# Query rows in tiles of the GLA stage, fetched a step ahead, and GLA keys turned through DRAM

## The chip, the cores and the metric

The kernel runs on one core of a Trainium2 chip. The metric is the device time of one execution in microseconds (us). Inputs and outputs are in DRAM, all in 32-bit floats.

## What is computed

One layer of a hybrid decoder for a prompt of 1024 tokens and, with the same weights, for eight decode queries ("samples") of one token each. One input projection feeds three branches; each is projected, gated, summed, and projected once more.

```python
h = rmsnorm(x, norm_gain)
proj = h @ w_in                     # 1024 x 10256
q, k, v, gla_g, a_lr, u, pool_g, xq, xg, merge = split(proj)
...
# A) gated linear attention, chunks of 64, 4 heads, key dim 128, value dim 256
q_dec, k_inv, k_end = qb * exp(b), kb * exp(-b), kb * exp(b_last - b)
att = where(mask, q_dec @ k_inv.T, 0)
o_intra, dS = att @ vb, k_end.T @ vb
S = decay * S + dS;  o = q_dec @ S_before + o_intra
# C) cross attention, 4 heads, head dim 256, 256 memory tokens
p = softmax((xq @ mk.T) * 256 ** -0.5);  o = p @ mv
```

For the prompt, the memory keys and values `mk`, `mv` are computed from `mem_prompt` and shared. For the samples each of the eight has its own keys and values in a cache, 256 tokens each per head. `k_end` is what the text calls the decayed keys: `dS` needs them with the token index on partitions, while the projection leaves them with the channel on partitions.

## The kernel before

**Main stream.** A product of two fp32 matrices is made of three fp32r matmuls of the parts "hi" and "lo" (`mm3`, L242 to L244; `split` makes the parts, hi on ScalarE, here ACT, L223, lo on VectorE, here DVE, L224). The input projection is cut in 40 pairs of 256 columns, each done by a Strassen-like scheme in seven products. A product has two halves, each of them twelve matmuls per group of 258 columns (tile `px`, six PSUM banks). Between the groups of the main stream the function `fill` may put side steps: first those of the memory keys, then the cross attention (`cross_steps`), then GLA (`gla_steps`), then pooling. A side step is what lies between two `yield`s; the number that it yields is its weight, and the weights are spread evenly over the main stream (WORK_A = 493 over about 330 places). So TensorE (PE) has one order, written out by hand, in which side steps and main groups alternate. SyncE (SP), which issues the loads, has program order too; the order of DVE, ACT and GpSimd (POOL) is set by a scheduler.

**Buffers.** Side matmuls write the tile `pz`, of which there are two PSUM banks. `R` is a ring of 14 tiles of 128x512 words for nearly all side data; `V` is a set of four such tiles; `raw` (three) takes the weights of the main stream from DRAM; `alc` and `st` are tiles of 128x256 words, two each, which the GLA stage uses for its gate input and its state.

**Samples in the cross stage.** `cross_sample` handles one head. `cross_scaled` and `cross_rows` turn the eight scaled queries and write them to DRAM (`xq_scr`). For each of four pairs of samples, `fetch` loads two tiles of keys `kc` (256 KB each) and a tile `qb` with the two query rows broadcast over all partitions, all from `V`. Four reduces on DVE (L777) multiply keys and row and sum them into `sc`. The next pair is fetched behind the reduces. Then `sc` is turned on TensorE (L791), the softmax makes `ps` (L793 to L798), `ps` is turned (L803) and copied into `pm`; two batches of four value tiles `vc` from `V` are multiplied by it (L817), the second loaded when the first has been used; the results are turned (`cs`).

The prompt's steps of the cross stage are `cross_memory` (turns the keys of a head, `mkT`, and splits the values), `cross_queries` (splits the queries, `xqs`), `cross_scores`, `cross_weights` (turns the weights, L724, and splits them, `pT`) and `cross_values`. `cross_steps` runs them over 16 chunks of 256 queries and takes one sub-step of the samples at each `yield next(samples, 0)`.

**GLA.** `gla_steps` runs over 16 chunks of 256 tokens (head h, chunk c), each in two parts of 128. `gla_load` fetches keys and queries two chunks ahead (`kq`), `gla_gates` makes the decayed keys (L935) and the other factors one chunk ahead, `gla_within` makes the masked 64x64 products of a part (L944, L945), turns the part's decayed keys on TensorE (L946) into the same bank, and splits both into `ak` (128x256, hi and lo). `gla_recur` multiplies `ak` with the values and updates the state (L963). The order within a chunk is: gates of the next one, within (even part), recur of the previous chunk's odd part, within (odd part), recur (even part), out.

Of the kernel before, what the change touches and what calls it, by code (L numbers as in the profile page):

```python
# [9 lines left out]
F32 = mybir.dt.float32  # L10
# [37 lines left out]
def trunk_kernel(ctx: ExitStack, tc: tile.TileContext,  # L48
# [159 lines left out]
    al_scr = scratch(2, "als", (P, HT))  # L208
    q_scr, k_scr = (scratch(2, s, PAIR) for s in ("qsc", "ksc"))
    vt_scr = scratch(NH, "vtsc", (T, DV))  # L210
    u_scr, xq_raw = (scratch(4, s, PAIR) for s in ("usc", "xqsc"))
    mix_scr = [None if n == 0 else scratch(4, f"mixsc{n}_", (P, 2, T)) for n in range(3)]
    on_scr = scratch(NH, "onsc", (DV // 32, 32, 2, 4, 2, 64))
# [539 lines left out]

    def cross_sample(h):

        if h == 0:
            cross_scaled(0)
            cross_rows(0)
            yield 1.2
            yield 0.5  # L760
            yield 0.5
        sc = wk.tile([P, 16], F32, tag="sc", name="sc", bufs=2)

        def fetch(b2):
            kc = [loaded(ck[2 * b2 + bb, :, h, :].rearrange("(a p) d -> p a d", p=P), [2, DV], "kc", V) for bb in range(2)]
            qb = V([2, DV], name="qb")
            nc.sync.dma_start(out=qb, in_=xq_scr[h][2 * b2:2 * b2 + 2].partition_broadcast(P))
            return kc, qb

        kcs, qb = fetch(0)  # L770
        yield 0.5
        yield 0.5
        for b2 in range(4):
            for bb in range(2):
                b, kc = 2 * b2 + bb, kcs[bb]
                for a in range(2):
                    nc.vector.tensor_tensor_reduce(kc[:, a, :], kc[:, a, :], qb[:, bb, :],  # L777
                                                   scale=1.0, scalar=0.0, op0=ALU.mult, op1=ALU.add,
                                                   accum_out=sc[:, a * NS + b:a * NS + b + 1])
            if b2 == 2 and h + 1 < NH:  # L780
                cross_scaled(h + 1)
            if b2 < 3:
                kcs, qb = fetch(b2 + 1)
                yield 1.2
            elif h + 1 < NH:
                cross_rows(h + 1)
            yield 1
# [44 lines left out]
    def cross_steps():  # L832
# [12 lines left out]

        samples = chain_of(cross_sample(h) for h in range(NH))
        cross_load(0)
        cross_memory(0)
        cross_fetch(0, 0)
        yield 2  # L850
        cross_queries(0, 0)
        cross_fetch(0, 1)
        for s in range(16 + 2):
            if s < 16:
                scores(s)
                yield 3
                if s + 1 < 16:
                    cross_queries(*divmod(s + 1, 4))
                if s + 2 < 16:
                    cross_fetch(*divmod(s + 2, 4))  # L860
            if s % 4 == 2 and s < 14:
                cross_load(s // 4 + 1)
            if s >= 1:
                yield next(samples, 0)
            if 0 <= s - 2:
                values(s - 2)
                yield 1.7
            if s >= 1:
                yield next(samples, 0)
            if s % 4 == 3 and s < 15:  # L870
                memory(s + 1)
                yield 2
            if 0 <= s - 1 < 16:
                weights(s - 1)
                yield 1.7
            for _ in range(3):
                if s >= 1:
                    yield next(samples, 0)
# [25 lines left out]
    def gla_gates(h, c):  # L904
# [29 lines left out]
        act(z, z, AF.Exp, scale=1.0 / TAU)  # L934
        nc.vector.tensor_tensor(k, k, z, op=ALU.mult)  # L935
        gla["g", h, c] = kq, kiqi, decp

    def gla_within(h, pr):

        c, cs = pr // 2, slice((pr % 2) * P, (pr % 2 + 1) * P)  # L940
        kq, kiqi, _ = gla["g", h, c]
        kt, qd, ki, qi = (x[:, cs] for x in (kq[:, 0], kq[:, 1], kiqi[:, 0], kiqi[:, 1]))
        t = PZ()
        nc.tensor.matmul(t[0:64, 0:P], lhsT=ki[:, 0:64], rhs=qi, start=True, stop=True)  # L944
        nc.tensor.matmul(t[64:P, 0:P], lhsT=ki[:, 64:P], rhs=qd, start=True, stop=True)  # L945
        nc.tensor.transpose(t[:, P:2 * P], kt, ident)  # L946
        nc.vector.copy_predicated(t[:, 0:P], nmask, zeros)
        ak = R([2, DV], F32R, name="ak")
        split(ak[:, 0], ak[:, 1], t[:, :DV])
        gla["w", h, pr] = ak[:, 0], ak[:, 1]  # L950

    def gla_recur(h, pr):
        c, cs = pr // 2, slice((pr % 2) * P, (pr % 2 + 1) * P)
        hi, lo = gla["w", h, pr]
        vh, vl = (x[:, pr % 2] for x in gla["vs", h, c])
        _, kiqi, decp = gla["g", h, c]
        st = gla.get(("st", h))
        t = PZ()
        td, to = t[:, :DV], t[:, DV:]
        mm3(td, hi[:, P:], lo[:, P:], vh, vl, True, True)  # L960
        mm3(to, hi[:, :P], lo[:, :P], vh, vl, True, st is None)
        if st is not None:
            nc.tensor.matmul(to, lhsT=kiqi[:, 1, cs], rhs=st, start=False, stop=True)  # L963
        s2 = wk.tile([P, DV], F32, tag="st", name="st", bufs=2)
# [104 lines left out]
    def gla_steps():  # L1069
# [7 lines left out]
        for n in range(N + 1):  # L1077
# [5 lines left out]
            if n < N:  # L1083
                gla_split(h, c)
                gla_within(h, 2 * c)
                yield 2
            if n > 0:
                gla_recur(ph, 2 * pc + 1)
                yield 2
                yield next(samples, 0)  # L1090
            if n < N:
                gla_within(h, 2 * c + 1)
                yield 2
                yield next(samples, 0)
# [471 lines left out]
```

## Time and profile before

| what | value |
| --- | --- |
| time, median of 3 runs | 1442.61 us (1440.45 to 1442.92) |
| time of the profiled run | 1445.01 us |
| its span, first to last instruction | 1443.3 us |
| mean granted TensorE clock | 0.997 |
| bytes moved by DMA | 259.42 MB, 180 GB/s on the mean |
| input projection with side steps | to about 1000 us |
| cross stage | about 120 to 380 us |
| GLA stage | about 385 to 740 us |
| transposes of decayed keys (L946) | 32, 10.5 us busy |

In the rows of the profile, a group or an instruction is named by its line, engine and operation, then by the tiles "out<-in"; `128*128 128x258` is a stationary operand of 128*128 and a moving one of 258 columns. What stands in brackets at a timeline row is the idle time of the engine ahead of it and what ended it. `SPq` is the queue in which SP issues DMAs, `PEld` the load of weights into TensorE. Rows of stretches give the window, its length, the busy time of PE, PEld, DVE, ACT and POOL with instruction counts, then the granted clock, the DMA share and GB/s. A row of waits gives the total, how often, and the longest. Tile rows give the shortest, median and longest duration in ns. DMA rows end with KB each and the median us from issue to landing.

### The profile page before, as it was taken

How to read it: one execution, taken by the hardware profiler on the slowest of the kernel's cores; microseconds unless marked ns; L12 is line 12 of the kernel's file. 1: busy time of each engine (PE TensorE's matmuls, PEld its weight loads, DVE VectorE, ACT ScalarE, POOL GpSimd, SP SyncE). 2: the span in 40 equal slices, each digit the busy share in tenths (PEclk: the TensorE clock that was granted, in tenths of full speed). 3: DMA queues.
4: the chain of work that ended last, by engine and by line, in shares of the span. 5: the costliest groups of instructions: out<-in, count | busy, mean ns of one | idle time of the engine just before them, and what ended most of it. 6: DMA issues, size and time to landing. Idle time of an engine off the chain costs nothing.

```text
span 1443.3 us, 28179 instructions
## 1 busy us (share of the span) xinstructions
PE 1417.4 (98%) x10689; PEld 1356.1 (94%) x10689; DVE 916.2 (63%) x2123; ACT 679.0 (47%) x1575; POOL 222.1 (15%) x401
## 2 busy tenths in 40 slices
PE   8999999999999999999999999999999999999998
PEld 6899999989899999999999999999999999999876
DVE  6954756666687777767766778785672434554436
ACT  6743544443465666656654445444472432233212
POOL 3211111124342121212221111111010000000000
PEclk9999999999999999999999999999999999999999
DMA  9355665656656363554654455454694777632633
GB/s 329 125 165 169 217 218 187 207 175 165 198 155 193 115 192 129 182 176 126 187 167 150 149 188 170 159 184 163 204 298 134 234 257 249 234 104 79 224 118 116
DMA packets 183507, 259.42 MB, mean 180 GB/s; under 512 B 22204, under 2 KB 132564, under 8 KB 183364
## 3 DMA queue, kind: packets, MB, share of 16 engines
q1 hardware_dynamic: 159900, 183.87, 41.5%
q0 software_dynamic: 23328, 73.56, 14.7%
q8 instruction: 84, 1.38, 0.4%
q14 instruction: 51, 0.42, 0.1%
q10 hardware_dynamic: 144, 0.20, 0.0%
HBM read 180.47 MB, written 77.56 MB: 179 GB/s over the span
## 4 chain that ended last, share of the span: by engine, by line
PE 88%; DMA 5%; DVE 5%; issue 1%; ACT 1%; SPq 0%; POOL 0%; DVEq 0%; ACTq 0%; POOLq 0%
PE px L242 25%; PE px L243 25%; PE px L244 25%; DMA qb<-xqs 3%; PE pz L244 2%; PE pz L243 2%; PE pz L242 2%; DMA raw<-in_w_in_dram 1%; DVE kc L777 1%; PE pz L963 1%; PE pz L404 1%; PE pz L944 1%; PE pz L817 1%; PE pz L946 1%; PE pz L907 0%
## 5 line engine op out<-in xcount | busy, mean ns | idle before, releaser
L244 PE MATMUL px<-bh,wbl 128*128 128x384 f32 (+1 forms) x576 | 184.1, 320 | 0.0
L243 PE MATMUL px<-bl,wbh 128*128 128x384 f32 (+1 forms) x576 | 184.1, 320 | 0.0
L242 PE MATMUL px<-bh,wbh 128*128 128x384 f32 (+1 forms) x576 | 183.7, 319 | 0.0
L554 ACT ACTIVATE r<-px 128x258 f32<-128x258 f32 x240 | 89.9, 375 | 47.4 <-PE px L244 46.9
L242 PEld LDWEIGHTS px<-bh,wbh 128*128 128x128 f32 x576 | 108.3, 188 | 0.0
L243 PEld LDWEIGHTS px<-bl,wbh 128*128 128x128 f32 x576 | 108.2, 188 | 0.0
L244 PEld LDWEIGHTS px<-bh,wbl 128*128 128x128 f32 x576 | 108.2, 188 | 0.0
L242 PE MATMUL px<-ot,s1h 128*128 128x258 f32 x320 | 94.1, 294 | 0.0
L242 PE MATMUL px<-o,a12h 128*128 128x258 f32 x320 | 93.4, 292 | 0.0
L242 PE MATMUL px<-ot,s3h 128*128 128x258 f32 x320 | 93.2, 291 | 0.0
L242 PE MATMUL px<-o,s4h 128*128 128x258 f32 x320 | 93.0, 291 | 0.2 <-DVE c L636 0.2
L242 PE MATMUL px<-o,a11h 128*128 128x258 f32 x320 | 92.8, 290 | 0.0
L242 PE MATMUL px<-ot,a22h 128*128 128x258 f32 x320 | 92.6, 289 | 0.0
L242 PE MATMUL px<-ot,s2h 128*128 128x258 f32 x320 | 92.2, 288 | 0.0
L243 PE MATMUL px<-o,a11h 128*128 128x258 f32 x320 | 91.1, 285 | 0.3 <-DVE o L224 0.3
L243 PE MATMUL px<-o,a12h 128*128 128x258 f32 x320 | 91.1, 285 | 0.0
L244 PE MATMUL px<-o,a12l 128*128 128x258 f32 x320 | 91.0, 284 | 0.0
L244 PE MATMUL px<-ot,s1l 128*128 128x258 f32 x320 | 90.9, 284 | 0.0
L243 PE MATMUL px<-ot,s1h 128*128 128x258 f32 x320 | 90.8, 284 | 0.0
L244 PE MATMUL px<-o,a11l 128*128 128x258 f32 x320 | 90.6, 283 | 0.0
L243 PE MATMUL px<-ot,s2h 128*128 128x258 f32 x320 | 90.1, 281 | 0.5 <-DVE ot L224 0.5
L243 PE MATMUL px<-ot,a22h 128*128 128x258 f32 x320 | 90.5, 283 | 0.0
(471 smaller groups left out, 4634.3 us busy)
## 6 DMA issues: line engine op xcount, KB each, us to landing
raw<-in_w_in_dram SPq DMA_DIRECT2D x80, 512.0 KB, 4.0
msc<-c POOLq DMA_DIRECT2D x24, 516.0 KB, 4.8
brsc<-c POOLq DMA_DIRECT2D x24, 516.0 KB, 3.7
sig<-msc SPq DMA_DIRECT2D x24, 516.0 KB, 6.0
brr<-brsc SPq DMA_DIRECT2D x48, 256.0 KB, 5.2
wbr<-in_w_branch_dram SPq DMA_DIRECT2D x24, 512.0 KB, 5.5
acc<-sig POOLq DMA_DIRECT2D x16, 516.0 KB, 5.2
acc<-acc SPq DMA_DIRECT2D x16, 516.0 KB, 7.0
```

The source lines that it names most:

```text
L242: nc.tensor.matmul(out, lhsT=lh, rhs=rh, start=start, stop=False, skip_group_check=more)
L243: nc.tensor.matmul(out, lhsT=lh, rhs=rl, start=False, stop=False, skip_group_check=more)
L244: nc.tensor.matmul(out, lhsT=ll, rhs=rh, start=False, stop=stop, skip_group_check=more)
L404: nc.tensor.matmul(t[:, :DV], lhsT=memT[k // 2][:, k % 2, a * P:(a + 1) * P], rhs=raw[k // 2][:, k % 2], start=k == 0, stop=k == NK - 1)
L554: nc.scalar.activation(r, acc[c][:, :QT], AF.Copy)
L777: nc.vector.tensor_tensor_reduce(kc[:, a, :], kc[:, a, :], qb[:, bb, :], scale=1.0, scalar=0.0, op0=ALU.mult, op1=ALU.add, accum_out=sc[:, ...
L817: nc.tensor.matmul(t[32 * j:32 * j + 32, :DV], lhsT=pm[:, a, 4 * i + j, :], rhs=vc[j][:, a, :], start=a == 0, stop=a == 1)
L944: nc.tensor.matmul(t[0:64, 0:P], lhsT=ki[:, 0:64], rhs=qi, start=True, stop=True)
L946: nc.tensor.transpose(t[:, P:2 * P], kt, ident)
L963: nc.tensor.matmul(to, lhsT=kiqi[:, 1, cs], rhs=st, start=False, stop=True)
```

## The change

**Samples.** The query rows `qb` are no longer one tile of `V` but two tiles of 128x256, taken from the tags `alc` and `st`, which the GLA stage uses later. `fetch` for the next pair is issued ahead of the reduces of the present one. `cross_scaled(0)` and `cross_rows(0)`, with the three yields behind them, leave `cross_sample` and stand at the front of `cross_steps`, which is rearranged there: both first query tiles are fetched first, and the second chunk's queries are split right behind the first scores. All later sub-steps of the samples stand some three positions earlier among the prompt's steps.

**GLA.** The transposes on TensorE (L946) are gone. `gla_gates` ends with one DVE transpose of the decayed keys (128x256, in blocks of 32x32) and four DMAs from POOL (32 KB each, in runs of 128 bytes), which put the blocks in order in a DRAM scratch `kt_scr`. `gla_turned` has SP load the turned keys (`ktr`, 128 KB) behind the chunk's first `gla_within`, and `gla_keys` splits them ahead of the second. `ak` now holds only the masked products, one ring tile per chunk.

```diff
     def cross_sample(h):
-        if h == 0:
-            cross_scaled(0)
-            cross_rows(0)
-            yield 1.2
-            yield 0.5
-            yield 0.5
...
-            qb = V([2, DV], name="qb")
-            nc.sync.dma_start(out=qb, in_=xq_scr[h][2 * b2:2 * b2 + 2].partition_broadcast(P))
+            qb = [wk.tile([P, DV], F32, tag=t, name="qb", bufs=2) for t in ("alc", "st")]
+            for bb in range(2):
+                nc.sync.dma_start(out=qb[bb], in_=xq_scr[h][2 * b2 + bb].partition_broadcast(P))
...
-        kcs, qb = fetch(0)
+        coming = fetch(0)
...
         for b2 in range(4):
+            kcs, qb = coming
+            coming = fetch(b2 + 1) if b2 < 3 else None
...
             if b2 < 3:
-                kcs, qb = fetch(b2 + 1)
                 yield 1.2
...
     def cross_steps():
         cross_load(0)
+        cross_fetch(0, 0)
+        cross_fetch(0, 1)
+        yield 1.5
         cross_memory(0)
-        cross_fetch(0, 0)
-        yield 2
         cross_queries(0, 0)
-        cross_fetch(0, 1)
+        yield 1.5
+        cross_scaled(0)
+        cross_rows(0)
+        yield 1
         for s in range(16 + 2):
             if s < 16:
                 scores(s)
+                if s == 0:
+                    cross_queries(0, 1)
                 yield 3
-                if s + 1 < 16:
+                if 0 < s < 15:
                     cross_queries(*divmod(s + 1, 4))
...
     def gla_gates(h, c):
+        kt = R([CT], name="kt")
+        nc.vector.transpose(kt, k)
+        for q in range(4):
+            nc.gpsimd.dma_start(out=kt_scr[4 * h + c][:, 32 * q:32 * q + 32].rearrange("(b r) k -> r b k", r=32),
+                                in_=kt[32 * q:32 * q + 32].rearrange("r (b k) -> r b k", k=32))
+    def gla_turned(h, c):
+        t = gla["kt", h, c] = R([2, 2, P], F32R, name="ktr")
+        nc.sync.dma_start(out=t[:, 0].bitcast(F32), in_=kt_scr[4 * h + c].rearrange("(j p) k -> p j k", j=2))
+    def gla_keys(h, c):
+        t = gla["kt", h, c]
+        split(t[:, 1], t[:, 0], t[:, 0].bitcast(F32))
     def gla_within(h, pr):
-        nc.tensor.transpose(t[:, P:2 * P], kt, ident)
-        ak = R([2, DV], F32R, name="ak")
-        split(ak[:, 0], ak[:, 1], t[:, :DV])
+        if pr % 2 == 0:
+            gla["ak", h, c] = R([2, 2, P], F32R, name="ak")
+        ak = gla["ak", h, c][:, pr % 2]
+        split(ak[:, 0], ak[:, 1], t[:, :P])
     def gla_recur(h, pr):
-        mm3(td, hi[:, P:], lo[:, P:], vh, vl, True, True)
+        mm3(td, kh, kl, vh, vl, True, True)
...
     def gla_steps():
                 gla_within(h, 2 * c)
                 yield 2
+                gla_turned(h, c)
             if n > 0:
                 gla_recur(ph, 2 * pc + 1)
...
             if n < N:
+                gla_keys(h, c)
                 gla_within(h, 2 * c + 1)
```

The order on SP before, at the fourth head's samples: keys `kc`, rows `qb`, the main stream's weights `raw`, then the values `vc`.

```order
L670 DMA kc<-in_cache_mem_k_dram 128x2x256 x2
L767 DMA qb<-xqs_127 128x512
L670 DMA kc<-in_cache_mem_k_dram 128x2x256 x2
L767 DMA qb<-xqs_127 128x512
L296 DMA raw<-in_w_in_dram 128x4x256
L670 DMA kc<-in_cache_mem_k_dram 128x2x256 x2
L767 DMA qb<-xqs_127 128x512
L670 DMA kc<-in_cache_mem_k_dram 128x2x256 x2
L767 DMA qb<-xqs_127 128x512
L296 DMA raw<-in_w_in_dram 128x4x256
L670 DMA vc<-in_cache_mem_v_dram 128x2x256 x8
```

The same place now:

```order
L671 DMA kc<-in_cache_mem_k_dram 128x2x256 x2
L763 DMA qb<-xqs_127 128x256 x2
L297 DMA raw<-in_w_in_dram 128x4x256
L671 DMA kc<-in_cache_mem_k_dram 128x2x256 x2
L763 DMA qb<-xqs_127 128x256 x2
L671 DMA kc<-in_cache_mem_k_dram 128x2x256 x2
L763 DMA qb<-xqs_127 128x256 x2
L297 DMA raw<-in_w_in_dram 128x4x256
L671 DMA kc<-in_cache_mem_k_dram 128x2x256 x2
L763 DMA qb<-xqs_127 128x256 x2
L297 DMA raw<-in_w_in_dram 128x4x256
L671 DMA vc<-in_cache_mem_v_dram 128x2x256 x8
```

Rows and keys of a pair stand one pair earlier against the `raw` loads, and there are two `qb` loads for each one of before.

On TensorE, at the fourth head's two batches of values, before: the first batch (rows `vc,pm`), one half of a product of the main stream (`px`, of whose twelve matmuls the first three stand here), then the prompt's `cross_values` (`pTh`, `pTl`); the second batch comes two halves further on.

```order
L817 MATMUL pz<-vc,pm 32x256 x8
L242 MATMUL px<-ot_752,s1h 128x258
L243 MATMUL px<-ot_753,s1h 128x258
L244 MATMUL px<-ot_752,s1l 128x258
...
L242 MATMUL pz<-pTh,mvsh 128x256
L243 MATMUL pz<-pTl,mvsh 128x256
L244 MATMUL pz<-pTh,mkv 128x256
```

Now one half lies between the two batches, and `cross_values` follows the second:

```order
L814 MATMUL pz<-vc,pm 32x256 x8
L243 MATMUL px<-ot_768,s1h 128x258
L244 MATMUL px<-ot_769,s1h 128x258
L245 MATMUL px<-ot_768,s1l 128x258
...
L814 MATMUL pz<-vc,pm 32x256 x8
```

The second batch moved ahead by two halves of a product. Counted in such halves from the start of the main stream, scores `sc`, `ps`, first and second batch of the third head stood at 115, 119, 120 and 126 and stand at 113, 114, 119 and 121; of the fourth head at 144, 146, 147 and 150, and now at 142, 144, 147 and 148. Of the first two heads, the two batches stood at 59 and 62, and at 89 and 94; now at 55 and 60, and at 87 and 91.

On SP where the GLA stage begins, now, with the new load `ktr` between a `raw` load and the loads two chunks ahead:

```order
L671 DMA v<-vtsc_162 128x2x256
L297 DMA raw<-in_w_in_dram 128x4x256
L948 DMA ktr<-ktsc_166 128x2x128
L901 DMA alc<-als_157 128x256
L904 DMA kq<-ksc_160 128x256
L904 DMA kq<-qsc_158 128x256
L671 DMA v<-vtsc_162 128x2x256
L297 DMA raw<-in_w_in_dram 128x4x256
L948 DMA ktr<-ktsc_167 128x2x128
L297 DMA raw<-in_w_in_dram 128x4x256
```

Without the two `ktr` rows this is the order of before. From the second chunk on, the buffer of `ktr` is one that the previous chunk's odd `gla_recur` frees.

More of the change, by code (lines that the diff above doesn't have):

```diff
@@ L210, in trunk_kernel @@
     vt_scr = scratch(NH, "vtsc", (T, DV))
+    kt_scr = scratch(4 * NH, "ktsc", (CT, P))
     u_scr, xq_raw = (scratch(4, s, PAIR) for s in ("usc", "xqsc"))
@@ L776, in cross_sample @@
                 for a in range(2):
-                    nc.vector.tensor_tensor_reduce(kc[:, a, :], kc[:, a, :], qb[:, bb, :],
+                    nc.vector.tensor_tensor_reduce(kc[:, a, :], kc[:, a, :], qb[bb],
                                                    scale=1.0, scalar=0.0, op0=ALU.mult, op1=ALU.add,
@@ L941, in gla_within @@
         kq, kiqi, _ = gla["g", h, c]
-        kt, qd, ki, qi = (x[:, cs] for x in (kq[:, 0], kq[:, 1], kiqi[:, 0], kiqi[:, 1]))
+        qd, ki, qi = (x[:, cs] for x in (kq[:, 1], kiqi[:, 0], kiqi[:, 1]))
         t = PZ()
@@ L945, in gla_within @@
         nc.tensor.matmul(t[64:P, 0:P], lhsT=ki[:, 64:P], rhs=qd, start=True, stop=True)
-        nc.tensor.transpose(t[:, P:2 * P], kt, ident)
         nc.vector.copy_predicated(t[:, 0:P], nmask, zeros)
-        ak = R([2, DV], F32R, name="ak")
-        split(ak[:, 0], ak[:, 1], t[:, :DV])
-        gla["w", h, pr] = ak[:, 0], ak[:, 1]
+        if pr % 2 == 0:
+            gla["ak", h, c] = R([2, 2, P], F32R, name="ak")
+        ak = gla["ak", h, c][:, pr % 2]
+        split(ak[:, 0], ak[:, 1], t[:, :P])
     def gla_recur(h, pr):
         c, cs = pr // 2, slice((pr % 2) * P, (pr % 2 + 1) * P)
-        hi, lo = gla["w", h, pr]
+        hi, lo = (gla["ak", h, c][:, pr % 2, i] for i in range(2))
+        kl, kh = (gla["kt", h, c][:, i, pr % 2] for i in range(2))
         vh, vl = (x[:, pr % 2] for x in gla["vs", h, c])
@@ L959, in gla_recur @@
         td, to = t[:, :DV], t[:, DV:]
-        mm3(td, hi[:, P:], lo[:, P:], vh, vl, True, True)
-        mm3(to, hi[:, :P], lo[:, :P], vh, vl, True, st is None)
+        mm3(td, kh, kl, vh, vl, True, True)
+        mm3(to, hi, lo, vh, vl, True, st is None)
         if st is not None:
```

## The prediction

> **What bounds the kernel now.** I began with the page's busy times, to see which engine sets the end. Then the table of stretches, to see where that engine is not full, and the waits of TensorE (PE), to see on what.
>
> ```profile
> PE 1417.4 (98%) x10689; PEld 1356.1 (94%) x10689; DVE 916.2 (63%) x2123; ACT 679.0 (47%) x1575; POOL 222.1 (15%) x401
> 350.00:400.00 50.00, 44.37 (x364) 40.92 (x363) 32.29 (x83) 20.85 (x49) 18.29 (x30) 0.97 0.60 166
> 400.00:450.00 50.00, 50.00 (x409) 47.83 (x408) 38.55 (x97) 31.40 (x88) 20.02 (x33) 1.00 0.62 179
> PE pz L803 <- DVE ps L798: 2.4, 1, 2.4
> PE pz L243 <- DVE pTl L224: 1.5, 1, 1.5
> PE pz L242 <- ACT xqsh L226: 1.4, 1, 1.4
> PE pz L244 <- DVE xq L227: 1.2, 2, 0.9
> PE pz L724 <- ACT xo L736: 1.1, 1, 1.1
> PE pz L817 <- DVE pm L804: 1.0, 1, 1.0
> PE pz L791 <- DVE mkTl L224: 1.0, 1, 1.0
> PE pz L242 <- DVE pTl L224: 1.0, 1, 1.0
> PE pz L1001 <- DVE ak L224: 0.7, 1, 0.7
> ```
>
> TensorE is busy for 1417.4 of 1443.3 us, so only two things can move the time: the work in its own queue, and the few places where it waits. The stretch from 400 to 450 us, in the GLA stage, has none (50.00 of 50.00); the stretch before it, where the cross stage ends, lacks 5.6 us. The first eight waits listed all lie in the cross stage and sum to 2.4 + 1.5 + 1.4 + 1.2 + 1.1 + 1.0 + 1.0 + 1.0 = 10.6 us; the ninth, 0.7 us, is the only one in GLA.
>
> The timeline of TensorE shows that some stalls cost more than their length.
>
> ```profile
> 122.57 0.38 PE L242 MATMUL pz<-mkTh,xqsh 128*128 128x256 f32 x1 [1.39 <-ACT xqsh L226]
> 124.77 0.42 PE L242 MATMUL px<-o,a12h 128*128 128x258 f32 x1
> 127.78 0.35 PE L244 MATMUL px<-o,a12l 128*128 128x258 f32 x1
> 366.58 0.39 PE L242 MATMUL px<-ot,s1h 128*128 128x258 f32 x1
> 368.90 0.42 PE L244 MATMUL px<-ot,s1l 128*128 128x258 f32 x1
> 119.03 0.28 PE L244 MATMUL px<-ot,a22l 128*128 128x258 f32 x1
> 119.15 0.60 PE L690 MATMUL pz<-ident,mkv 128*128 128x128 f32 x4
> 119.50 0.36 PE L242 MATMUL px<-ot,a22h 128*128 128x258 f32 x1
> ```
>
> One step of the main stream is 0.12 us (119.03 to 119.15), so the twelve products of half a product, after which a side step may follow, take 1.43 us; I call that a slot. Behind the stalls that end at 122.57 the stream goes at half rate: 14 steps from 124.77 to 127.78 take 3.01 us in place of 1.68, 1.3 us lost. Behind the 2.4 us stall, 11 steps from 366.58 to 368.90 take 2.32 us in place of 1.32, 1.0 us lost. The cross stage so has 10.6 + 2.3 = 12.9 us to give, no more.
>
> **Part 1, the query rows a step ahead.** Where the wait for `ps` comes from is read from VectorE's (DVE's) waits and SyncE's (SP's) timeline.
>
> ```profile
> DVE kc L777 <- DMA qb<-xqs: 24.2, 11, 4.1
> 349.32 0.34 SPq L767 DMA_DIRECT2D qb<-xqs  x1
> 355.06 0.42 DVE L777 CUSTOM_DVE_ANT_0 kc<-kc,qb 128x256 f32<-128x256 f32 x1 [4.10 <-DMA qb<-xqs]
> ```
>
> The query rows are issued behind the keys whose buffers the last reduces free, land 5.7 us later, and VectorE stands for 4.1 us at them; the stalls of 1.5 (`pTl`), 1.1 (`xo`) and 2.4 us (`ps`) on TensorE follow before 366.58, in VectorE's order. With the rows a step ahead in buffers of their own this goes: 5.0 us, and the 1.0 us at half rate. The order of the changed kernel puts issue and first reduce mostly three to six slots apart (4.3 to 8.6 us); for the few that stand two apart I leave 0.5 us.
>
> The other cross stalls (1.4, 1.2, 1.0, 1.0, 1.0, and 1.3 at half rate) hang on which side step stands next to which, and every step of the samples moves up by some three positions. So the old ones go, 6.9 us, and new neighbours come. At the start, the turned memory keys and the first scores still stand one slot apart, but the split of the queries is issued earlier: of 2.6 us I leave half, 1.3 us (0.8 to 2.2).
>
> The other neighbours are read from the order: sample scores, the turn of the weights `ps`, and two batches of values `vc`. The third head now has scores and `ps` one slot apart, and its second `vc` batch two slots behind its first; the fourth has its second batch one slot behind. These are the rows that price them.
>
> ```profile
> 364.69 0.40 DVE L793 TENSOR_REDUCE nm<-pz 8x1 f32<-8x256 f32 x1
> 365.90 0.34 DVE L798 TENSOR_SCALAR ps<-ps,sm 8x256 f32<-8x256 f32 x1
> vc<-in_cache_mem_v_dram SPq DMA_DIRECT2D x32, 256.0 KB, 4.1
> 183.44 1.07 PE L817 MATMUL pz<-vc,pm 128*32 128x256 f32 x16
> 184.52 3.52 SPq L670 DMA_DIRECT2D vc<-in_cache_mem_v_dram  x4
> 190.99 0.57 PEld L817 LDWEIGHTS pz<-vc,pm 128*32 128x32 f32 x10 [0.48 <-DMA vc<-in_cache_mem_v_dram]
> ```
>
> From `nm` to the end of `ps` is 1.55 us, with the two transposes and signals ahead some 2.3; TensorE is there after 1.7 us or less: 0.8 us (0.5 to 1.3).
>
> The second batch uses the four buffers of the first, so its loads start when the first has been multiplied: 1.08 us after its start here (184.52 against 183.44). Four issues of 0.34 us and a landing of 4.1 us put the last tile at 1.08 + 1.4 + 4.1 = 6.6 us; in the case shown, where the issues took 3.52 us, TensorE had the last tile at 191.47, 8.0 us. One slot behind its first batch TensorE arrives at 1.07 + 1.43 = 2.5 us and waits 4.1 us; two slots behind, with four transposes between, at 4.2 us, and waits 2.4 us. Since first tiles can be used while the last lands, 0.5 us less is possible, and by the 8.0 us 1.4 more. Before, all four heads had these batches three or more slots apart, and only that 0.48 us was lost. After each I add a half-rate stretch as after the 2.4 us stall: 1.0 us, and 1.3 us for the longer one.
>
> **Part 2, GLA keys through DRAM.** It takes 32 transposes of 128x128 out of TensorE's queue.
>
> ```profile
> L946 PE MATMUL pz<-ident,kq 128*128 128x128 f32 x32 | 10.5, 329 | 0.0
> 392.44 0.33 PE L946 MATMUL pz<-ident,kq 128*128 128x128 f32 x1
> 392.74 0.28 PE L243 MATMUL px<-ot,s2h 128*128 128x258 f32 x1
> ```
>
> The group's 10.5 us overlap their neighbours. Four transposes in a row moved the stream from 119.15 to 119.50, 0.09 us each; a single one with one main step behind it took 392.44 to 392.74, 0.30 less a step of 0.12, which is 0.18. I take the first, 32 x 0.09 = 2.8 us, since part of the other is the change of mode, which stays for the products next to it; the upper end is 5.8 us. The Trainium skill (TensorE: Matmul & The Clock Gate, Part 4: PE-mode transpose) gives about 275 ns for a transpose within a kernel. By that page, as an estimate, 8.8 us would go, 6.0 more than I take; the trace speaks against it.
>
> What comes in its place runs beside TensorE, unless the keys are late.
>
> ```profile
> 389.47 0.40 DVE L935 TENSOR_TENSOR kq<-kq,bz 128x256 f32<-128x256 f32 x1
> 398.56 0.28 PE L242 MATMUL pz<-vsh,ak 128*128 128x256 f32 x1
> L590 POOL DMA_DIRECT2D vtsc<-vt x64 | 41.3, 655 | 32.1 <-DVE vt L587 27.2 <-DVE bz L932 4.1 <-issue 0.7
> vtsc<-vt POOLq DMA_DIRECT2D x64, 64.0 KB, 3.1
> kq<-ksc SPq DMA_DIRECT2D x16, 128.0 KB, 3.9
> L223 ACT ACTIVATE ak<-pz x32: 358/383/387, 395.7 to 731.3; 128x256 fp32r<-128x256 f32 x32
> 431.93 0.28 PE L242 MATMUL pz<-vsh,ak 128*128 128x256 f32 x1
> 439.47 0.28 PE L242 MATMUL pz<-vsh,ak 128*128 128x256 f32 x1
> ```
>
> VectorE gains 16 turns of 128x256 (about 0.4 us each) and GpSimd (POOL) 64 issues of some 0.65 us; with VectorE at 38.55 and POOL at 20.02 of 50 us this is covered. The shorter `ak` splits pay for most of the new `ktr` splits.
>
> First chunk: the decayed keys are ready at 389.9, turned at 390.3, four writes issued by 392.8, landed near 395.5 to 395.9 (3.1 us, for twice the bytes), read back 3.9 us later, split in 0.38 us on ACT and as much again on VectorE: about 400.2. TensorE wants them at 398.6: 1.6 us (0.5 to 3.5). The 0.7 us stall on `ak` there goes.
>
> Later chunks: the writes are a chunk ahead, but the load of `ktr` takes a ring buffer that TensorE frees in the odd recurrence of the chunk before. SP stands there until then; behind it the order has loads for the next chunk and for products still ahead, which I cost at nothing: what covers them is that they are asked for a chunk or a product early, and a late one would cost TensorE what it is late. From 431.93: 0.6 us to the release, 0.4 issue, 3.9 landing, 0.8 split, and about 1.2 for the `ak` split that stands behind it on ACT and VectorE, whose two queues are held meanwhile. That is 6.9 us against 439.47 - 431.93 = 7.5. The margin of 0.6 us is under the scatter of such loads, so I put 0.1 us on each of 14 chunks and round up: 1.6 us (0 to 8).
>
> **The sum.** Gone: 10.6 + 2.3 + 0.7 + 2.8 = 16.4 us. New: 1.3 (start) + 0.5 (rows) + 0.8 (`ps`) + 2.4 + 1.0 (third head's values) + 4.1 + 1.3 (fourth head's) + 1.6 + 1.6 (keys) = 14.6 us. The profiled run of 1445.0 us becomes 1443.2. It lies 2.4 us over the median of the three runs, 1442.6, so the forecast is 1440.8, rounded 1441.
>
> **The rivals.** *Values hidden* (faster). If the two late batches find their tiles, because TensorE reaches them later in time than the slots say, or the loads land early, 8.8 us of the new costs go: 1432, and 1436 if only half do. For it: the stream loses time at other places too. Against it: the order has one slot where the loads need 6.6 us. 0.28.
>
> *Dear transposes* (faster). If a transpose costs TensorE the 0.275 us that the page gives, the result is 1435. Against it the two marginal costs above; 0.06.
>
> *Keys late in every chunk* (slower). If `ktr` lands later than about 4.5 us, the margin of 0.6 us is used up and TensorE stands at each of 14 even recurrences. At a landing of 5.0 us that is 14 x 0.5 = 7 us, less the 1.6 counted: 1446; at 5.5, 14 x 1.0: 1453. For it: the load is held until a buffer frees, and nothing covers it then. Against it: the 3.9 us row, for a load of the same size. The Trainium skill (VectorE: DVE Perf Modes, Rules for kernel authors) says to turn 128x128 on TensorE where the result may go to PSUM, as it may here. By that rule the change goes the wrong way, as this rival has it; no trace yet shows the detour. 0.18.
>
> *The rows still late* (slower). SP works in order, and a fetch ahead stands behind keys that wait for their buffers. If the rows land no earlier than before, 5.0 + 1.0 - 0.5 = 5.5 us stay: 1446. Against it: two buffers more for the rows, and four for keys alone. 0.06.
>
> **The numbers.** A difference of 0.2% (1439.7 to 1445.5) is about what a measurement of this kernel can tell from no change. The forecast of no change has 0.42, faster 0.28 + 0.06 = 0.34, slower 0.18 + 0.06 = 0.24. The range: down 8 us, about the values' whole price or the transposes' upper end and the keys' lower ends (3.0 + 1.1 + 1.6) with half a batch; up 8 us, the keys late by 0.6 us per chunk. 1433 to 1449.
>
> **What would show it.** Right: VectorE's wait for `qb` falls from 24.2 us to a few; TensorE's waits for `ps`, `pTl` and `xo` near 356 to 366 are gone, and in their place are one of about 4 us on `vc` near 370 and one of about 2 near 312; the first recurrence waits 1 to 2 us on `ktr`; the stretch from 350 to 400 still lacks some 5 us. Wrong: no wait on `vc` over 1 us (first rival); TensorE under 49.5 of 50 us in each stretch from 400 to 700 (third); VectorE's `qb` wait over 15 us (fourth).

## The result, and the profile after

The changed kernel takes 1457.94 us (median of 4 runs, 1454.01 to 1461.75) against 1441.94 for the kernel before: a ratio of 1.0107 [1.0089, 1.0124]. It is 16 us slower, outside the range given. The profiled execution took 1457.84 us (span 1456.0), 12.8 more than the profiled one of before.

The page's busy times and the same stretches as before (stretch; busy us of PE, PEld, DVE, ACT, POOL with counts; granted clock, DMA share, GB/s):

```profile
PE 1419.2 (97%) x10657; PEld 1354.6 (93%) x10657; DVE 921.0 (63%) x2155; ACT 680.3 (47%) x1591; POOL 257.3 (18%) x465
350.00:400.00 50.00, 43.13 (x352) 39.03 (x352) 32.93 (x85) 21.16 (x50) 18.79 (x32) 1.00 0.56 154
400.00:450.00 50.00, 48.86 (x391) 45.98 (x390) 36.37 (x96) 28.56 (x81) 27.76 (x48) 1.00 0.63 177
450.00:500.00 50.00, 43.71 (x343) 41.19 (x343) 34.69 (x95) 28.19 (x83) 12.18 (x22) 0.93 0.46 140
```

TensorE has 32 instructions fewer (the transposes) and yet 1.8 us more busy time, and the GLA stage, full before, lacks 6.3 us between 450 and 500. TensorE's waits (total, times, longest), then VectorE's and SP's:

```profile
PE px L243 <- DVE c L620: 6.3, 1, 6.3
PE pz L800 <- DVE ps L795: 3.8, 2, 2.3
PE pz L1018 <- DVE ak L225: 3.4, 1, 3.4
PE pz L814 <- DMA vc<-in_cache_mem_v_dram: 2.5, 3, 1.2
PE pz L1080 <- ACT os L1074: 1.5, 1, 1.5
PE pz L243 <- ACT ktr L224: 0.7, 1, 0.7
```
```profile
DVE kc L775 <- DMA qb<-xqs: 15.8, 9, 3.8
SPq L948 <- PE pz L245: 72.7, 10, 10.4
```

The largest two, `c` at 6.3 and `ak` at 3.4 us, are in no term of the forecast. The `ktr` that I had priced at 3.2 us costs 0.7, though SP's queue stands 72.7 us in front of its loads.

Where the time goes is read by following the same products of the main stream through both traces. The lag is a product's start in the other trace less its start in before's (products that start in before at the time heading the column; us):

| kernel | 309.7 | 394.6 | 409.9 | 466.9 | 820.8 |
|---|---|---|---|---|---|
| after | -1.5 | -0.9 | 1.7 | 11.6 | 12.7 |
| e1 query rows alone | 0.2 | -0.1 | -0.1 | 0.4 | 4.0 |
| e2 GLA keys alone | -2.5 | -2.8 | -0.2 | 9.5 | 10.8 |
| e6 reading alone | -3.3 | -5.0 | -5.1 | -4.8 | -6.6 |
| e9 GLA keys, late writes | -3.0 | -1.5 | 2.3 | 8.1 | 9.1 |
| e13 turn, no tile | -2.2 | -1.1 | -0.5 | -0.5 | -0.6 |
| e14 tile, no turn | -0.5 | -0.5 | 3.4 | 3.8 | 5.8 |
| e15 keys, no tile | -3.7 | -5.2 | -4.6 | 6.0 | 4.6 |
| e17 no tile, late writes | -2.1 | -3.1 | -2.5 | 3.9 | 4.5 |
| e16 e17 and e8 together | -9.9 | -10.5 | -8.2 | -6.8 | -4.3 |

Against this profile of before the cross stage comes out about even, as forecast. The loss is made in two places of the GLA stage: 2.6 us around 400, and 9.9 us between 410 and 467. Kernels with before's cross stage reach the second column as much as 5 us early, and the profiled runs lie apart as other runs do (that of before 2.4 us over its median, that of e15 4.6 under its own). So single lags there mean little, and only the steps between neighbouring columns are read below.

### The profile page after: what moved, and what is told of

It reads as the page before. It is cut to its first block, busy times and chain, and to the rows that moved or that the text cites. A ratio compares the mean times of both kernels' runs of the same rounds, so it can differ in the third digit from the quotient of the medians.

```text
span 1456.0 us, 28374 instructions
## 1 busy us (share of the span) xinstructions
PE 1419.2 (97%) x10657; PEld 1354.6 (93%) x10657; DVE 921.0 (63%) x2155; ACT 680.3 (47%) x1591; POOL 257.3 (18%) x465
## 4 chain that ended last, share of the span: by engine, by line
PE 84%; DVE 6%; DMA 5%; ACT 2%; issue 2%; SPq 1%; POOL 0%; DVEq 0%; ACTq 0%
PE px L243 25%; PE px L244 24%; PE px L245 24%; PE pz L245 2%; PE pz L244 2%; PE pz L243 2%; DMA qb<-xqs 2%; DMA raw<-in_w_in_dram 1%; DMA s<-in_state_gla_dram 1%; PE pz L960 1%; DMA x<-in_x_prompt_dram 1%; PE pz L980 1%; PE pz L814 1%; DVE ws L306 1%; DMA vc<-in_cache_mem_v_dram 1%
## 5 line engine op out<-in xcount | busy, mean ns | idle before, releaser
L243 PE MATMUL px<-ot,s1h 128*128 128x258 f32 x320 | 93.5, 292 | 0.0
L245 PE MATMUL px<-ot,s3l 128*128 128x258 f32 x320 | 90.4, 282 | 0.0
```

Of the source, the lines that this page charges most:

```text
L243: nc.tensor.matmul(out, lhsT=lh, rhs=rh, start=start, stop=False, skip_group_check=more)
L245: nc.tensor.matmul(out, lhsT=ll, rhs=rh, start=False, stop=stop, skip_group_check=more)
```

## The experiments

My theories at the outset: that SP, standing at the `ktr` loads, holds back the loads behind it (the third rival in another guise); against it, that the added writes or the added tile upset VectorE's and GpSimd's queues; and for the cross stage, that new neighbours in the order, not the fetch ahead, cost what it gains. The ratios below are against the kernel before, timed on the same chip.

**The two halves.** e1 has the query rows alone (the hunks of `cross_sample` and of the cross stage), e2 the GLA keys alone (all others).

> Only the samples' half of the change: query rows in their own tiles and a step ahead, and the front of the cross steps; the GLA stage is that of before. Theory A (the loss comes from the load of the turned keys, at which SyncE stands, so that the sample states behind it land late and hold ScalarE and VectorE): without that load the profile's lag of 8 us near 452 to 468 us goes, and the 2.5 us at the first chunk too; 1437 to 1443 us against 1442. Rival B (the loss comes from the samples' steps standing three positions earlier, in the cross stage and behind it): 1450 us or more.

> Only the GLA half: decayed keys turned on VectorE and through DRAM; the cross stage is that of before. Theory A: 1450 to 1458 us, with a stall of several us on TensorE that ends with VectorE's evictions, behind ScalarE's wait for the sample states. Rival B: 1439 to 1443 us, the 32 transposes saved less a little. If the two halves' losses sum to much less than 16 us, it is their meeting that costs.

e1 took 1446.38 us, 1.0028 [1.0018, 1.0038]: 3.6 us slower, between the two ranges. e2 took 1457.12, 1.0102 [1.0088, 1.0116]: 14.4 us, nearly the whole, and in theory A's range. By the lags the cross stage of e1 is even (-0.1 us by 394.6, within the scatter told above), and its loss is one stall near the end of the GLA stage, with half-rate steps behind it:

```profile
749.05 1.08 PE L1065 MATMUL pz<-ident,os 128*128 128x128 f32 x4 [2.06 <-ACT os L1059]
750.15 0.42 PE L243 MATMUL px<-ot,s1h 128*128 128x258 f32 x1
752.73 0.34 PE L243 MATMUL px<-ot,s1h 128*128 128x258 f32 x1
```

Twelve steps from 750.15 to 752.73 take 2.58 us in place of 1.43. With 2.06, and some 0.6 on the transposes and the step ahead, that is 3.8 us; the lag grows by 3.6 from 466.9 to 820.8. Before had no stall of that kind in this stage.

**The neighbours put back.** e4 is e1 with the samples' steps at their old places, three positions later; e8 is e4 with one number of the planner's pace changed too.

```diff
+    if h == 0:
+        yield 0.5
+        yield 0.5
+        yield 0.5
     coming = fetch(0)
-WORK_A, WORK_B = 493.0, 108.0     # e8 only
+WORK_A, WORK_B = 494.3, 108.0     # e8 only
```

> The samples' half alone, with three empty sub-steps ahead of the first head, so that the samples' steps stand again where they stood before against the prompt's steps (third head: scores 116, ps 120, values 121 and 127; fourth: 145, 147, 148, 151), while the rows stay a step ahead. Theory V (in the cross stage the gain of the rows is eaten by new neighbours, ps one slot behind the scores and the second batch of values one or two slots behind the first): 5 to 8 us faster than the samples' half alone, 1432 to 1437 us. Rival N (neighbours don't matter, the rows alone do): within 2 us of the samples' half alone.

> The samples' half with the three sub-steps that put them at their old places, and the planner's sum of work raised from 493.0 to 494.3, which is what these sub-steps and the new front add, so that side steps end where they ended before. In the run without it, 3 us were lost near 745 us, where the last steps of the samples stood close together (a stall of 1.8 us on os). If that is the cause: 1434 to 1437 us, against 1438 without. If the steps' places in the cross stage move and meet other neighbours: 1438 us or more.

e4 took 1438.22 us, 0.9972 [0.9961, 0.9983], and e8 1437.02, 0.9960 [0.9946, 0.9975], the fastest kernel of this study; e4 lies 1.2 us over the range expected, e8 at the slow end of its own. With its steps held in place the samples' half is 4 to 6 us faster than before; letting them slide by three costs some 8 us (1446.38 - 1438.22), more than the gain. The gain is not the fetch ahead's alone, since e4 and e8 also have the new front of `cross_steps`: at the product that starts at 135.05 us in before, with the same side steps done, e8 is already 4.2 us ahead and e4 2.7, while their first reduce of sample keys comes only at 142 and 144 us. The fetch ahead without the new front was not tried. Nor is the stall on `os` what parts e1 from e4: e4 has it too (1.8 us). It is gone in e8, which has a wait of 2.4 us for `alc` near 599 instead. The stretch from 280 to 320 us, first of after, then of e8, shows what the slide costs:

```profile
280.00:320.00 40.00, 36.04 (x285) 32.95 (x286) 20.98 (x44) 18.25 (x46) 8.84 (x15) 0.96 0.49 154
```
```profile
280.00:320.00 40.00, 40.00 (x348) 38.33 (x348) 25.72 (x56) 18.52 (x44) 10.14 (x18) 1.00 0.65 199
```

With the third head's steps apart again TensorE is full and the clock is whole. VectorE still waits 11.0 us for `qb` in e8, and yet `ps`, `pTl` and `xo` are no longer among TensorE's waits; one of 2.1 us on `vc` stands there.

**The GLA half in two.** e5 has the turn and the four writes alone; TensorE still makes the transposes. e6 has the reading alone: no turn and no writes, `ktr` loaded from other data of the same size, so its keys are not the decayed ones.

```diff
+    kt = R([CT], name="kt")                       # e5: before plus these
+    nc.vector.transpose(kt, k)
+    # and the four writes of the change
-    in_=kt_scr[4 * h + c].rearrange("(j p) k -> p j k", j=2)      # e6: e2 without the above, and
+    in_=vt_scr[h][c * CT:(c + 1) * CT, :P].rearrange("(j p) k -> p j k", j=2)
```

> The kernel before, with only the writing side of the GLA half added: one VectorE transpose of the decayed keys per chunk and four DMAs on GpSimd that put them in DRAM, where nothing reads them; the transposes on TensorE stay. Theory A (the reading side costs: SyncE stands at the load until the chunk before frees a ring tile, and ScalarE and VectorE stand at the split): within 3 us of before. Rival P (the writing side costs: four more issues per chunk on GpSimd push its large writes of the main stream into the loads of the sample states, and ScalarE, VectorE and then TensorE stand): 6 to 12 us slower than before, with the stall near 460 us.

> The GLA half without its writing side: no VectorE transpose of the keys, no writes; the load of ktr takes as many bytes of the values' scratch instead, and the state of GLA is computed from those, not from the keys. Theory A: 1450 us or more, with the stall of 6 us near 460. Rival P: 1439 to 1446 us, that stall gone; in both the first chunk's stall (3.3 us on ak) goes, since nothing has to be written first.

e5 took 1460.14 us, 1.0114 [1.01, 1.0128]: 17.4 slower, more than rival P's 6 to 12. e6 took 1442.31, 0.9993 [0.9984, 1.0003]: no difference, with all 16 loads of `ktr` on SP, which stands 40.3 us at them, and their splits. The theory of SP's standing queue fell; the loss is on the writing side. e6 also bounds the gain from the 32 transposes: with the loads and splits in their place, nothing that can be measured.

**Two attempts at the read.** e3 is the changed kernel with `ktr` in two buffers of its own and 29 input tiles for 30; e7 is e2 with `ktr` loaded by GpSimd (KTR stands for the source, unchanged).

```diff
-    t = gla["kt", h, c] = R([2, 2, P], F32R, name="ktr")                  # e3; and NE = 29
+    t = gla["kt", h, c] = shaped(wk.tile([P, 512], F32R, tag="ktr", name="ktr", bufs=2), [2, 2, P])
-    nc.sync.dma_start(out=t[:, 0].bitcast(F32), in_=KTR)                   # e7
+    nc.gpsimd.dma_start(out=t[:, 0].bitcast(F32), in_=KTR)
```

> The whole change, but the turned keys ktr have two tiles of their own in place of a ring tile (the space is taken from the tiles of the input, 29 for 30), so that their load waits for no recurrence of the chunk before. Theory A: SyncE's 72.7 us of waiting at that load go, the states come earlier, the 6.3 us stall and its half-rate stretch are gone: 1444 to 1450 us. Rival R (ring pressure by kt and ktr as such, or late landings, not SyncE's standing): 1455 us or more, the stall stays.

> The GLA half with the load of ktr issued by GpSimd in place of SyncE, so that SyncE never stands at it. If SyncE's standing is what delays the sample states (theory A in its narrow form), the stall near 460 us goes: 1444 to 1450 us. If not, 1455 us or more; GpSimd then stands at the ring tile instead, and its own writes come later.

e3 took 1520.2 us, 1.0529 [1.0506, 1.0552]: the missing input tile costs time from 131 us on, long before `ktr`, so the run says nothing on it. e7 took 1481.84, 1.0271 [1.0257, 1.0284]. There TensorE stands at `ktr` in six of the 16 chunks, first for 7 us. What GpSimd does ahead of that first load stands below it:

```profile
406.28 0.58 PE L243 MATMUL pz<-vsh,ktr 128*128 128x256 f32 x1 [6.97 <-ACT ktr L224]
```
```profile
397.73 5.13 POOL L591 DMA_DIRECT2D vtsc<-vt  x8
402.86 0.72 POOL L946 DMA_DIRECT2D ktr<-ktsc  x1
```

It is not as I had expected: GpSimd does not stand at the ring tile, for none of its 16 loads has a pause ahead of it. The load itself is late, because its turn comes behind eight stores of `vt`; in e2 SP issues it at 391.49, 11 us earlier. On SP the waiting load showed no cost (e6); on GpSimd the kernel takes 25 us more than e2.

**What the tile costs.** Four kernels are before with a piece of the writing side. e10: the turn into a ring tile, no writes. e13: the turn into `z` (half of a `bz` tile), dead by then. e14: the tile, with a copy of one column in place of the turn. e11: e5 with one write of 128 KB, its layout not that of the turned keys.

```diff
+    kt = R([CT], name="kt"); nc.vector.transpose(kt, k)                    # e10
+    nc.vector.transpose(z, k)                                              # e13
+    kt = R([CT], name="kt"); nc.vector.tensor_copy(kt[:, 0:1], k[:, 0:1])  # e14
-    # the four writes                                                      # e11
+    nc.gpsimd.dma_start(out=kt_scr[4 * h + c].rearrange("t k -> (t k)").rearrange("(p n) -> p n", p=P), in_=kt)
```

> The kernel before with only the VectorE transpose of the decayed keys added, 16 of 0.44 us into a ring tile that nothing reads; no DMA. Theory Q: the stall near 460 us is not there, 1442 to 1447 us, with the first chunk's 3.3 us on ak if VectorE's order makes it. Rival T (the turn and its ring tile do the harm, by VectorE's order): 1452 us or more.

> The kernel before with the VectorE transpose of the decayed keys added, but into the half of the gates' own tile that is dead by then, so that no ring tile more is taken; nothing reads it. Theory L (the ring tile costs, by the order and the waits that it makes): 1441 to 1445 us, the 3.3 us on ak in the first chunk back to under 1. Rival T (the transpose's own 0.44 us on VectorE, 16 times, costs): 1449 to 1452 us, as with a tile of its own.

> The kernel before with only the ring tile: per chunk one more tile of the ring, into which VectorE copies a single column of the keys, and which nothing reads. Theory L: 1447 to 1452 us, as with the transpose. Rival T: 1441 to 1445 us.

> The writing side alone as in the run with four writes (1460 us), but one DMA per chunk, 128 KB in 1-KB runs in the order in which VectorE leaves the blocks, which nothing reads. Theory Q, if the issues' own time counts: 4 x 0.58 us become one, 1446 to 1452 us. Theory Q, if the standing at the turned keys counts: 1455 us or more, since one DMA stands there as four did. Rival D: 1442 to 1447 us, since the small runs are gone.

e10 took 1450.65 us, 1.0059 [1.004, 1.0079]; e14 1450.34, 1.0052 [1.0035, 1.0069]; e13 1443.92, 1.0005 [0.9991, 1.0018]; e11 1452.12, 1.0066 [1.0047, 1.0085]. e10 lies between its two ranges, e11 at the edge of one. The 16 turns cost nothing that can be measured. The tile alone, with hardly an instruction to fill it, costs 7.0 us: one buffer more per chunk from the ring that `kq`, `bz`, `v` and `ak` share. VectorE's timeline at the start of the GLA stage shows where, first e13, then e14, with TensorE's stall in its last row:

```profile
386.54 0.47 DVE L892 TENSOR_SCALAR bz<-pz,vec 128x256 f32<-128x256 f32 x1
389.52 0.68 DVE L225 TENSOR_TENSOR s3l<-ws,s3h 128x512 fp32r<-128x512 f32 x1
390.80 0.70 DVE L588 STREAM_TRANSPOSE vt<-c 128x512 f32<-128x512 f32 x1
395.86 0.74 DVE L225 TENSOR_TENSOR ak<-pz,ak 128x256 fp32r<-128x256 f32 x2
```
```profile
387.92 0.69 DVE L225 TENSOR_TENSOR s3l<-ws,s3h 128x512 fp32r<-128x512 f32 x1 [0.21 <-ACT s3h L224]
389.28 0.47 DVE L892 TENSOR_SCALAR bz<-pz,vec 128x256 f32<-128x256 f32 x1
396.43 1.30 DVE L588 STREAM_TRANSPOSE vt<-c 128x512 f32<-128x512 f32 x2
398.21 0.75 DVE L225 TENSOR_TENSOR ak<-pz,ak 128x256 fp32r<-128x256 f32 x2
398.78 0.38 PE L1004 MATMUL pz<-ident,smp 128*8 128x128 f32 x2 [3.03 <-DVE ak L225]
```

The order itself is another one. With the tile, the second chunk's gates (`bz` from `pz`) stand behind `s3l`, 2.7 us later, and the turns of `vt` behind the whole gate chain, so `ak` is split 2.4 us later. TensorE stands there 3.03 us in e14, 3.28 in e10 and 3.38 in after, against 1.30 in e13 and 0.62 in e6. These are the 2.6 us around 400. Of the rest of the 7.0 the largest piece is a stall of 1.6 us at 647.72. Why one buffer more gives this order lies in the scheduler's plan, which no trace shows. With one write in place of four e11 loses 10.4 us and e5 17.4, for the same bytes; whether it is the number of issues or the 128-byte pieces of the four is not told apart.

**What the writes cost.** e18 is e5 without the tile (turned into `z`), e15 is e2 without the tile. e9 is e2 with the four writes of a chunk moved behind the even recurrence of the chunk before; e17 is e9 without the tile.

```diff
-    kt = R([CT], name="kt")
+    kt = z                                    # e15, e17, e18
     gla_recur(h, 2 * c)                       # e9, e17: the four writes, as gla_store
     yield 2
+    if n + 1 < N:
+        gla_store(*divmod(n + 1, 4))
```

> The kernel before with the turn in the dead half of the gates' tile (1444 us alone) and the four writes to DRAM where the change has them, which nothing reads; the transposes on TensorE stay. Theory Q: the event near 455 us is there, 1450 to 1456 us. Rival (it needs the read-back): 1443 to 1446 us.

> The whole GLA half of the change with its four writes and the load, but turned into the dead half of the gates' tile. Theory L: the GLA half loses 14 us with the tile; about 8 to 9 of them go, 1445 to 1450 us, and what is left is GpSimd's four issues. If the tile is all of it: 1440 to 1444 us. Rival T: 1455 us or more.

> The GLA half, with the four writes of the turned keys issued later in the program, behind the even recurrence in place of the end of the gates, so that GpSimd takes the states' writes and the main stream's large write ahead of them. Theory Q (GpSimd stands at the turned keys with those writes behind it, and they then fall on the loads of the next states): the 6 us stall near 460 us and its half-rate stretch go, 1446 to 1450 us; the 3.3 us on ak in the first chunk stays. Rival D (the traffic of many 128-byte runs as such): 1454 us or more.

> The GLA half with the turn in the dead half of the gates' tile and the four writes behind the even recurrence. Theory Q (GpSimd's order makes the event near 455 us): it goes, and the half is within 4 us of before, 1441 to 1446 us. Rival: the read-back or the splits make it, 1450 us or more.

e18 took 1450.79 us, 1.0061 [1.0046, 1.0075]; e15 1454.29, 1.008 [1.0059, 1.0102]; e9 1453.89, 1.0084 [1.006, 1.0109]; e17 1448.31, 1.0043 [1.0031, 1.0055]. e18 lies in theory Q's range; e15 and e9 lie some 4 us over the ranges of their theories, and e9 at the edge of rival D's. By e18 less e13, the four early writes cost 8.6 us without any tile. Their main place is the 6.3 us stall. In the timeline of after it is followed back from TensorE over VectorE and ACT to SP and GpSimd:

```profile
439.90 2.33 POOL L943 DMA_DIRECT2D ktsc<-kt  x4 [4.94 <-DVE rq L264]
442.36 0.72 POOL L594 DMA_DIRECT2D usc<-c  x1
442.71 0.47 SPq L671 DMA_DIRECT2D s<-in_state_gla_dram  x1
443.07 0.73 POOL L1049 DMA_DIRECT2D out_dram<-s  x1
443.93 0.56 POOL L594 DMA_DIRECT2D usc<-c  x1
449.66 0.91 ACT L1047 ACTIVATE s<-s,as 128x256 f32<-128x256 f32 x2 [3.08 <-DMA s<-in_state_gla_dram]
451.66 0.88 DVE L1048 SCALAR_TENSOR_TENSOR s<-vb,smp,s 128x256 f32<-128x256 f32 x2 [4.36 <-ACT r L555]
452.57 0.37 SPq L671 DMA_DIRECT2D s<-in_state_gla_dram  x1
456.12 0.51 ACT L1047 ACTIVATE s<-s,as 128x256 f32<-128x256 f32 x1 [3.84 <-DMA s<-in_state_gla_dram]
461.98 0.58 PE L243 MATMUL px<-o,a11h 128*128 128x258 f32 x1 [6.29 <-DVE c L620]
462.36 0.42 PE L244 MATMUL px<-o,a11h 128*128 128x258 f32 x1
464.51 0.42 PE L245 MATMUL px<-o,a11l 128*128 128x258 f32 x1
```

The same place in before:

```profile
431.21 0.71 POOL L1032 DMA_DIRECT2D out_dram<-s  x1
438.87 0.59 POOL L593 DMA_DIRECT2D usc<-c  x1
439.51 0.48 SPq L670 DMA_DIRECT2D s<-in_state_gla_dram  x1
444.58 0.51 ACT L1030 ACTIVATE s<-s,as 128x256 f32<-128x256 f32 x1 [1.23 <-DMA s<-in_state_gla_dram]
451.86 0.28 PE L242 MATMUL px<-o,a11h 128*128 128x258 f32 x1
```

In before the state's store leaves at 431.21, 8.3 us ahead of the next load of `s`. In after GpSimd stands 4.94 us at VectorE (whose turn of `kt` ends at 439.61), then issues four writes, and the stores of `c` and `s` queued behind leave at 442 to 444, right upon that load. ACT starts on `s` 6.95 us after the load's issue, in place of 5.07, and waits 3.08 and 3.84 us; VectorE waits 4.36 for ACT; the evictions of `c` in VectorE's queue are late, and TensorE stands 6.29 us. Its next ten steps go at half rate (462.36 to 464.51). That these stores slow the load itself is read from the rows and was not tried alone; that the early writes bring the event about is shown. It is there with early writes without the tile too, first in e15, then in e18:

```profile
455.68 0.58 PE L243 MATMUL px<-o,a11h 128*128 128x258 f32 x1 [6.86 <-DVE c L620]
```
```profile
456.20 0.58 PE L243 MATMUL px<-o,a11h 128*128 128x258 f32 x1 [5.21 <-DVE c L620]
```

It is in neither kernel with late writes (e9, e17). But these only put smaller stalls in its place: by the lags, the stretch from 410 to 467 still costs 5.8 us in e9 and 6.4 in e17, against 9.7 in e2 and 10.6 in e15. I expected e17 within 4 us of before, and it is 6.7 slower. Its largest stalls on TensorE in that stretch:

```profile
423.96 0.67 PE L908 MATMUL pz<-alc,w 128*128 128x256 f32 x2 [1.10 <-DMA alc<-als]
432.54 0.39 PE L243 MATMUL pz<-vsh,ktr 128*128 128x256 f32 x1 [1.58 <-DVE bz L892]
441.19 0.38 PE L243 MATMUL pz<-vsh,ktr 128*128 128x256 f32 x1 [0.92 <-ACT ktr L224]
```

Which edit each of these hangs on I did not settle, so the traffic of the small writes, whenever they come (rival D), is not excluded as the cause of this rest. Nor do the prices found one by one add up in the GLA half: e2 loses 14.4 us; without the tile it is 10.9 (e15), with late writes 12.2 (e9), with both 6.7 (e17). These 6.7 us stay open. They are not fixed either: in e16, below, which has the same GLA half behind another cross stage, the stretch from 410 to 467 costs 1.4 us.

**Both mended.** e12 is e8 with the GLA keys as in e9; e16 the same as in e17.

> The whole change with both mends: the samples' steps back at their places with the sum of work to match (1437 alone) and the late writes in GLA. Theory Q and the neighbours: the samples' half keeps its 5 to 6 us, the GLA half costs what it costs alone with late writes: 1440 to 1445 us. If the halves meet elsewhere: 1450 us or more.

> Both halves mended: the samples' steps at their places with the sum of work to match, the writes later, and the turn without a tile of its own. Theory L: 1436 to 1441 us, no better than the samples' half alone (1437), since the read-back and the dropped transposes came out even. Rival T: 1443 us, as with the tile.

e12 took 1443.39 us, 1.0016 [1.0002, 1.003]; e16 1439.26, 0.9979 [0.9969, 0.9989], slightly faster than before; both are in the ranges expected. e8, without any of the GLA keys, is ahead of it by its ratio (0.9960), though the intervals touch.

## Why the prediction was wrong, point by point

**The bound.** Right: only TensorE's queue and its waits count, and all of the loss is found there.

**The rows a step ahead.** Half right. The waits for `pTl` and `xo` near 356 to 366 went, but one for `ps` is still there, 1.5 us of the 2.4. The wait for `qb` fell only from 24.2 to 15.8 us, over the sign that I had set for the fourth rival. Its longest piece ends at 349.98, 7 us ahead of that stall, and from there VectorE works with hardly a pause until `ps` is done:

```profile
349.98 0.43 DVE L775 CUSTOM_DVE_ANT_0 kc<-kc,qb 128x256 f32<-128x256 f32 x1 [3.84 <-DMA qb<-xqs]
358.52 0.26 PE L800 MATMUL pz<-ident,ps 8*128 8x8 f32 x2 [1.52 <-DVE ps L795]
```

So at the fourth head the rows were still late, as the fourth rival has it, and at a smaller price than its 5.5 us. A wait of VectorE counts only through TensorE's: e8 has 11.0 us of it and none of these stalls. The start has some 1.0 us left (1.3 forecast).

**The late values.** Right in the waits, not in what I added behind them. TensorE's timeline in after, third and fourth head:

```profile
309.70 0.62 PE L814 MATMUL pz<-vc,pm 128*32 128x256 f32 x2
313.11 0.39 PE L243 MATMUL px<-ot,s3h 128*128 128x258 f32 x1
365.06 1.07 PE L814 MATMUL pz<-vc,pm 128*32 128x256 f32 x16
372.53 0.39 PE L243 MATMUL px<-ot,s3h 128*128 128x258 f32 x1
```

The third head's second batch takes 3.41 us in place of 1.07: 2.3 lost (2.4 forecast). From the fourth head's first batch to the main stream behind its second go 7.47 us in place of 1.07 + 1.43 + 1.07 = 3.6: 3.9 lost (4.1 forecast). The wait near 370 is in pieces, none over 1.2 us. The half-rate stretches of 1.0 and 1.3 us did not come: a few steps behind 313.11 and 372.53 TensorE is at 0.12 us a step. So the late values cost 6.2 us for 8.8 forecast. The first rival, values hidden, fell with it.

**`ps` and the evictions.** Too small: 3.8 us in two waits, 2.3 at the third head and 1.5 at the fourth, for 0.8 in one; and behind the first, 15 steps at half rate (294.86 to 298.07) cost 1.4 more. And a wait for `os` at the end of the GLA stage, 1.5 us in after, 2.1 in e1, was in no term: TensorE reaches a side step whose ACT work was just in time before. By the lags it makes up e1's loss.

**The transposes.** 2.8 us were to go; e6, with loads and splits in their place, lies between 2.3 us faster and 0.4 slower than before. That leaves no room for the second rival's 8.8 us, unless the reading eats them, for which its trace has only 0.3 us of waiting at `ktr`. What the transposes cost alone was not tried, and no run shows that part of the 0.18 us of a single one is a change of mode, as I put it.

**Keys late.** The sum had 1.6 us for the first chunk and 1.6 for the others; `ktr` stalls 0.7 us in all, and the first recurrence, which was to wait 1 to 2 us, does not wait for it behind the 3.4 us on `ak`. The DMA table and the groups of after have the load and the writes:

```profile
ktr<-ktsc SPq DMA_DIRECT2D x16, 128.0 KB, 2.2
```
```profile
L943 POOL DMA_DIRECT2D ktsc<-kt x64 | 37.2, 589 | 90.5 <-DVE kt L941 73.0 <-DVE c L646 6.6 <-DVE pz L962 5.9
```

The load lands after 2.2 us, not the 3.9 of the `kq` row that I took. The third rival's mechanism fell, though its side of the result came true: TensorE was short in some stretches for other reasons.

**The step that failed** is "with VectorE at 38.55 and POOL at 20.02 of 50 us this is covered", and beside it "The 0.7 us stall on `ak` there goes". I priced the turns and the writes by a share of busy time. The turns were free (e13). But the turned keys needed a ring tile, which moved VectorE's order at the start of the stage and made the `ak` stall 3.4 us in place of 0.7 (e14: 7 us over the whole kernel). And the writes' 64 issues, 37.2 us of GpSimd's time, were covered in sum, but GpSimd stands 73.0 us in order for `kt` ahead of them, and the stores behind them, as the rows above have it, then fall on a load that the path needs (e18: 8.6 us over e13). Each added alone to before, these are about 16 us together, near what e5 lost (17.4). In the GLA half with its reading they overlap with costs that I did not take apart: 6.7 of e2's 14.4 us are left without tile and early writes.

## What to carry to other kernels

A queue with time to spare is no cover: ask what stands ahead of the new instruction and what behind it, and on whose transfer that will fall once it is late. A new buffer from a shared ring can have a price even if hardly anything fills it; try the work in a dead buffer first. When a change makes one engine fetch earlier, see that the steps behind it do not slide into new neighbours: here the same half was worth 4 to 6 us with the steps held in place, and cost 3.6 without.

## What the runs showed of the hardware

A waiting load on SP showed no cost: e6, where SP stood 40.3 us at `ktr`, came out at 0.9993. A load of 128 KB landed in 2.2 us (`ktr`) where another of that size took 4.6 in the same kernel (`kq`; 3.9 in before), so the size alone did not set it. A load of the state was in use 7 us after its issue, in place of 5, when four writes were issued in the 3 us ahead of it and three stores within 1.3 us of it; which of them did it was not tried. Half rate followed stalls from 1.39 us (before, 14 steps at 0.215 us) to 6.29 us (after, ten such steps) without growing with them, and it did not follow each: behind the 3.38 us on `ak` in after the granted clock from 390 to 410 us stays at 1.00.
